# Two RWKV head pairs in one block of the mixer stage, with HGRN on single buffers

## Chip, core and metric

The kernel runs on one core of a Trainium2 chip. The metric is the device time of one execution in microseconds (us); three executions of the kernel before took 3644.89, 3647.28 and 3647.89 us. TensorE (PE) multiplies, VectorE (DVE), ScalarE (ACT) and GpSimd (POOL) work on elements, SyncE (SP) and ScalarE issue most of the transfers. Each engine takes its instructions in program order and waits on semaphores for the others.

## What is computed

One layer of a streaming encoder over 2048 prompt tokens and, with the same weights, 32 sample tokens: a normalised input times one wide weight matrix, whose columns feed three groups of heads side by side (RWKV-7, forgetting attention, HGRN2), then an output projection and a feed-forward network. The change concerns the RWKV group: four heads of 64 channels, whose state is carried from token to token.

```python
xs = p + mu * (p_prev - p)
r, k, v, wl, al, gl = jnp.split(xs, RW_SPLITS, axis=-1)
w = jnp.exp(-jnp.exp(-softplus(-(w0 + tanh(wl) @ w2)) - 0.5))
a = sigmoid(a0 + al @ a2)
g = sigmoid(gl) @ g2
kk = k * k_k, normalised per head
k = k * (1.0 + (a - 1.0) * k_a)
# for each token:
S = S * w_t - (S @ kk_t) (kk_t * a_t) + v_t k_t
y_t = S @ r_t
# then: normalise y per head, add the bonus (r . k . r_k) v, multiply by g
```

(The lines above are shortened from the reference; the transposes and casts are left out.) HGRN2, with four heads too, carries a state in the same way, with a decay per channel and without the correction by `kk`.

## The kernel before

**Stages.** `project_and_recur` runs first, up to about 1300 us: the input projection, the two recurrences, and small work that is strewn in. Behind it stand the attention, the output projection and the feed-forward network, which the change doesn't touch.

**Projection.** Each f32 factor is split into two parts, so a product is three matmuls (L360, L361, L362, tile `ip_p`), 128x128 weights against 256 tokens. The weights arrive as `w_st` (L314, queue of SyncE, two buffers), and are split into `w_hi` (L316, ScalarE) and `w_lo` (L318, GpSimd or VectorE). Results go to the scratch `cm` in HBM, row per channel, column per token. The recurrences read them from there.

**RWKV in half blocks.** `rwkv_block` handles 128 tokens (two chunks of 64) of one pair of heads: 128 partitions are two heads of 64 channels. It is a generator of 34 steps, so that other work can stand between the steps. It loads r, k, v with one extra column and mixes neighbouring tokens (`shifted`, tiles `rw_raw`, `rw_t`, three buffers for `rw_raw`); makes decay and gates from the low-rank tile `rl_e`, which the first pair makes for both (`rwkv_lora`, L1088); takes a running sum (L1111) and exponentials; builds the scaled tiles `rw_G` and `rw_kb`; multiplies them into `rw_gm` (L1151); and inverts a triangular 64x64 matrix per head and chunk, in five levels. At each level a burst of small matmuls (L1201) goes to PSUM, ScalarE copies it to `rw_x` (L1205), a second burst (L1210) uses it, VectorE writes the halves into `rw_tt` under a mask (L993) and transposes to `rw_tn` (L1214), which the next level reads. Then come `rw_wu` (L1221, L1224), `rw_rp` (L1229, L1231), `rw_q` (L1238), the state step per chunk (L1245, L1247), and the output with three sums over heads by the matrix `bones` (L1266, L1272, L1280). All RWKV matmuls write `rw_ps`, three PSUM banks in turn. Nearly all bursts use a part of the array of 64 rows and 64 columns, one part for each head.

**HGRN.** `hgrn_block` handles 256 tokens of one pair in 13 steps. Its tiles `hg_q`, `hg_k`, `hg_b`, `hg_w`, `hg_att`, `hg_vt` have two buffers each, the temporary `hg_t` five.

**Order.** `interleave` takes, again and again, the job with the smallest due time, runs it to its next `yield` and adds the job's step to its due time. A block starts at its number `n`, and takes `RW_LEN / RW_STEPS` units per step; so about three half blocks are under way at a time, each at another step. The projection of the next rounds is a job too and stands between them. The tile framework then sets each engine's order by its own estimate, and puts a semaphore wherever a buffer must come free or a value must be there.

Of the kernel before, what the change touches and what calls it, by code (L numbers as in the profile page):

```python
# [10 lines left out]
F32 = mybir.dt.float32  # L11
# [7 lines left out]
SEQ = 2048  # L19
NS = 32  # L20
# [994 lines left out]
def shifted(K, rp, row, t0, T, n, mu, first, name, bufs=3):  # L1015

    nc = K.nc
    raw = rp.tile([128, T + 1], F32, name="rw_raw", bufs=3)
    if first is None:
        nc.sync.dma_start(out=raw[:, 0:n + 1], in_=K.cm[row:row + 128, t0 - 1:t0 + n])  # L1020
    else:
        if first == 0:
            nc.gpsimd.memset(raw[:, 0:1], 0.0)
        else:
            nc.sync.dma_start(out=raw[:, 0:1], in_=K.a["state_rwkv_shift"][0, 0, 0, row:row + 128].rearrange(
                "(p o) -> p o", o=1))
        nc.sync.dma_start(out=raw[:, 1:n + 1], in_=K.cm[row:row + 128, t0:t0 + n])
    if t0 + n in (SEQ, TOK):
        j = (row - RW0) // 128 + (7 if t0 + n == TOK else 0)
        nc.gpsimd.tensor_copy(K.last[:, j:j + 1], raw[:, n:n + 1])  # L1030
    d = rp.tile([128, T], F32, name="rw_t", bufs=6)
    nc.gpsimd.tensor_tensor(d[:, :n], raw[:, 0:n], raw[:, 1:n + 1], ALU.subtract)
    x = rp.tile([128, T], F32, name=name, bufs=bufs)
# [32 lines left out]
def rwkv_block(K, rp, pp, p, t0, T, n, first, loras, st, yrow):  # L1066
# [10 lines left out]
    if p == 0:  # L1077
        loras[t0] = rwkv_lora(K, rp, t0, T, n, first)
        yield
    lora = loras[t0]  # L1080
    xr = shifted(K, rp, RW0 + 128 * p, t0, T, n, vec(K, "rw_mu", p), first, "rw_r")
    xk = shifted(K, rp, RW0 + 256 + 128 * p, t0, T, n, vec(K, "rw_mu", 2 + p), first, "rw_k")
    xv = shifted(K, rp, RW0 + 512 + 128 * p, t0, T, n, vec(K, "rw_mu", 4 + p), first, "rw_v")
    cs = slice(128 * p, 128 * p + 128)

    def gate(i, bias, name):
        ps = pt()
        nc.tensor.matmul(ps[:, :T], lhsT=K.lw[:, i, cs], rhs=lora, start=True, stop=True)  # L1088
        g = sb(name)
        if bias is None:  # L1090
            nc.scalar.activation(g, ps[:, :T], AF.Copy)
            return g
        nc.vector.tensor_scalar(g, ps[:, :T], bias, -40.0, ALU.add, ALU.max)
        nc.scalar.activation(g, g, AF.Exp, scale=-1.0)
        nc.scalar.activation(g, g, AF.Ln, bias=c1)
        return g

    yield
    nl = gate(0, vec(K, "rw_w0", p), "rw_nl")
    nc.scalar.activation(nl, nl, AF.Exp, scale=-1.0, bias=K.eps_c[:, 2:3])  # L1100
    if n < T:
        nc.gpsimd.memset(nl[:, n:], 0.0)
    yield
    av = gate(1, vec(K, "rw_a0", p), "rw_a")
    nc.scalar.activation(av, av, AF.Exp, scale=-1.0)
    gv = gate(2, None, "rw_g")
# [15 lines left out]
    kk = sb("rw_kk")  # L1122
    nc.scalar.activation(kk, xk, AF.Square, scale=vec(K, "rw_k_k", p))
    ps = pt()
    nc.tensor.matmul(ps[:, :T], lhsT=K.bones, rhs=kk, start=True, stop=True)
    rn = sb("rw_t", bufs=6)
    nc.vector.tensor_scalar(rn, ps[:, :T], 1.0e-24, None, ALU.max)
    nc.scalar.activation(rn, rn, AF.Ln, scale=float(2.0 ** 20))
    nc.scalar.activation(rn, rn, AF.Exp, scale=-0.5, bias=K.rwc[:, 0:1])
    nc.vector.scalar_tensor_tensor(kk, xk, vec(K, "rw_k_k", p), rn, ALU.mult, ALU.mult)  # L1130
    yield

    G = rp.tile([128, 3, NCH, 64], F32, name="rw_G", bufs=3)
# [8 lines left out]
    nc.vector.tensor_scalar(kp, av, vec(K, "rw_k_a", p), K.ka1[:, p:p + 1], ALU.mult, ALU.add)  # L1142
# [6 lines left out]
    for c in range(NCH):  # L1149
        for ps, h in zip(gps, hs):  # L1150
            nc.tensor.matmul(ps[:, 128 * c:128 * c + 128], lhsT=kb[h, c, :, :], rhs=G[h, 0:2, c, :], start=True, stop=True)  # L1151
    for ps in gps:
        v = ps[:, :128 * NCH].rearrange("p (c x) -> p c x", x=128)
        g = rp.tile([128, NCH, 192], F32, name=f"rw_gm{len(gm)}", bufs=2)
        mask = K.m_up.rearrange("p a b -> p (a b)")[:, None, :].broadcast_to([128, NCH, 128])
        nc.vector.tensor_tensor(g[:, :, 0:128], v, mask, ALU.mult)
        gm.append(g)
        if len(gm) == 1:
            m0 = rp.tile([64, NCH, 64], F32, name="rw_m0", bufs=2)
            nc.scalar.activation(m0, g[64:, :, 0:64], AF.Copy)  # L1160
        yield

    kf = kb.rearrange("p c a t -> p c (a t)")
    nc.gpsimd.tensor_tensor(kf, kf, ch(w)[:, :, 63:64].broadcast_to([128, NCH, 128]), ALU.mult)
    ps = pt()
    for c in range(NCH):
        nc.tensor.transpose(ps[:, 128 * c:128 * c + 128], kf[:, c, :], K.ident)
    for i in range(2):
        nc.scalar.activation(gm[i][:, :, 128:192], ps[:, :128 * NCH].rearrange("p (c h x) -> p c h x", h=2, x=64)[:, :, i],
                             AF.Copy)  # L1170
    mt = [m0, gm[1][64:, :, 0:64]]
    kn = rp.tile([128, NCH, 2, 64], F32, name="rw_kn", bufs=2)
    tt = rp.tile([128, NCH, 64], F32, name="rw_tt", bufs=3)
    tn = rp.tile([128, NCH, 64], F32, name="rw_tn", bufs=2)
    flat = lambda t: t.rearrange("p c t -> p (c t)")
    to_tokens(K, pt(), G[:, 0], [kn[h, c, 0, :] for c in range(NCH) for h in hs])
    nc.gpsimd.tensor_copy(tt, K.i2[:, None, :].broadcast_to([128, NCH, 64]))
    for h, m in zip(hs, mt):
        for c in range(NCH):
            by_level(K, tt[h, c, :], 1, halves(m[:, c, :], 1, 1)[:, None], h)  # L1180
    nc.vector.transpose(tn, tt)
    yield

    wu = rp.tile([128, 2, NCH, 2, 64], F32, name="rw_wu", bufs=2)
    to_tokens(K, pt(), ch(xv), [wu[:64, :, c, 1, :] for c in range(NCH)])
    yield

    ps = pt()
    for c in range(NCH):
        for i, h in enumerate(hs):  # L1190
# [962 lines left out]
```

## Time and profile before

| | |
|---|---|
| median of three executions | 3647.28 us |
| profiled execution, whole | 3650.61 us |
| its span, first to last instruction | 3648.6 us |
| instructions | 62814 |
| TensorE busy | 3454.1 us (95%) |
| VectorE busy | 1917.3 us (53%) |
| ScalarE busy | 1486.8 us (41%) |
| GpSimd busy | 1376.2 us (38%) |
| mean granted clock of TensorE | 0.978 |

A row of a group names line, engine, operation, written and read tiles, shape and count; behind the first bar stand the busy time in us and the mean in ns of one, behind the second the idle time of the engine before them and what ended it. A row of waits has the waiting line, what ended the wait, the total in us, how often, and the longest. A row of the timeline has start and duration in us. Matmuls overlap, so the durations of neighbours add up to more than the time that passes.

### The profile page before, as it was taken

The numbers are of one execution on the slowest core, as the hardware profiler recorded it, in microseconds if no ns is written. First come the engines' busy times: TensorE is split into PE (matmuls) and PEld (weight loads), VectorE is DVE, ScalarE is ACT, GpSimd is POOL, SyncE is SP. The second block draws the span as 40 slices with busy tenths as digits, with TensorE's granted clock in tenths as the row PEclk, the third lists the DMA queues.
The fourth block names the chain that finished last, engine by engine and source line by source line (L and its number), as shares of the span: only waits on it lengthen the run. The fifth ranks groups of instructions, "written<-read, shape, count | busy, mean of one in ns | idle before, by whom it ended". The sixth has DMA issues, their size and how long they took to land.

```text
span 3648.6 us, 62814 instructions
## 1 busy us (share of the span) xinstructions
PE 3454.1 (95%) x24242; PEld 2893.4 (79%) x24242; DVE 1917.3 (53%) x4445; ACT 1486.8 (41%) x3492; POOL 1376.2 (38%) x1608
## 2 busy tenths in 40 slices
PE   7999999999999998999999999899999999999999
PEld 5988888888778865666666666688999998998998
DVE  3456667566676555666666655532333345233336
ACT  4356556556566554444444433322122213211212
POOL 5434444344344323544443443333223333322223
PEclk9999999999999999999999999999999999999999
DMA  6433334324533344422222214533222232211212
GB/s 206 144 116 103 96 107 132 119 80 136 185 117 90 103 131 139 124 73 60 75 67 63 75 44 112 176 129 96 63 64 76 71 95 96 70 58 47 70 58 95
DMA packets 363647, 361.37 MB, mean 99 GB/s; under 512 B 36511, under 2 KB 305396, under 8 KB 362292
## 3 DMA queue, kind: packets, MB, share of 16 engines
q1 hardware_dynamic: 325216, 320.02, 29.1%
q10 hardware_dynamic: 37748, 37.29, 3.3%
q8 instruction: 191, 3.13, 0.4%
q14 instruction: 108, 0.88, 0.1%
q0 software_dynamic: 384, 0.05, 0.0%
HBM read 291.14 MB, written 66.14 MB: 98 GB/s over the span
## 4 chain that ended last, share of the span: by engine, by line
PE 72%; DVE 7%; POOL 6%; ACT 6%; DMA 5%; issue 4%; ACTq 0%; SPq 0%; POOLq 0%; DVEq 0%
PE ff_p L1814 8%; PE ff_p L1813 8%; PE ff_p L1812 8%; PE ff_o L1764 4%; PE ff_o L1763 4%; PE ff_o L1762 4%; PE pb_pv L690 4%; PE ip_p L360 3%; PE ip_p L361 3%; PE ip_p L362 3%; PE pb_sc L643 2%; PE pb_ps L706 2%; PE op_p L1672 1%; PE op_p L1671 1%; PE op_p L1670 1%
## 5 line engine op out<-in xcount | busy, mean ns | idle before, releaser
L1813 PE MATMUL ff_p<-h_lo,wih 128*128 128x384 f32 (+2 forms) x1760 | 623.5, 354 | 0.1
L1812 PE MATMUL ff_p<-h_hi,wih 128*128 128x384 f32 (+2 forms) x1760 | 621.6, 353 | 1.9 <-ACT wih L1698 0.8
L1814 PE MATMUL ff_p<-h_hi,wil 128*128 128x384 f32 (+2 forms) x1760 | 622.0, 353 | 1.1 <-POOL wil L1699 1.1
L1699 POOL TENSOR_TENSOR wil<-ff_st,wih 128x1024 fp32r<-128x1024 f32 x134 | 322.3, 2405 | 582.1 <-ACT wih L1698 563.5
L360 PE MATMUL ip_p<-h_hi,w_hi 128*128 128x256 f32 (+1 forms) x1472 | 442.2, 301 | 14.2 <-ACT h_hi L296 5.4
L361 PE MATMUL ip_p<-h_lo,w_hi 128*128 128x256 f32 (+1 forms) x1472 | 429.6, 292 | 4.1 <-POOL h_lo L297 1.9
L362 PE MATMUL ip_p<-h_hi,w_lo 128*128 128x256 f32 (+1 forms) x1472 | 428.3, 291 | 0.3 <-DVE w_lo L318 0.3
L1812 PEld LDWEIGHTS ff_p<-h_hi,wih 128*128 128x128 f32 x1760 | 331.8, 189 | 17.9 <-ACT wih L1698 1.0
L1814 PEld LDWEIGHTS ff_p<-h_hi,wil 128*128 128x128 f32 x1760 | 333.3, 189 | 14.8 <-POOL wil L1699 1.4
L1813 PEld LDWEIGHTS ff_p<-h_lo,wih 128*128 128x128 f32 x1760 | 332.1, 189 | 14.4 <-POOL h_lo L1887 0.6
L1699 POOL TENSOR_TENSOR wol<-ff_st,woh 128x1024 fp32r<-128x1024 f32 x66 | 162.0, 2459 | 406.0 <-ACT woh L1698 405.7
L700 POOL TENSOR_TENSOR fx_acc<-fx_acc,fx_pt 128x512 f32<-128x512 f32 (+3 forms) x176 | 206.5, 1188 | 268.6 <-PE pb_pv L690 152.1
L360 PEld LDWEIGHTS ip_p<-h_hi,w_hi 128*128 128x128 f32 x1472 | 283.6, 193 | 27.5 <-ACT h_hi L296 6.0
L1821 DVE TENSOR_TENSOR ff_sg<-ff_sg,ff_p 128x384 f32<-128x384 f32 (+2 forms) x110 | 64.5, 586 | 458.2 <-PE ff_p L1814 458.0
L1768 DVE TENSOR_TENSOR acc<-acc,ff_o 128x512 f32<-128x512 f32 (+1 forms) x306 | 208.7, 684 | 173.1 <-PE ff_o L1764 172.6
L1762 PE MATMUL ff_o<-woh,act_h 128*128 128x512 f32 (+1 forms) x724 | 286.7, 396 | 10.1 <-ACT act_h L1822 7.2
L361 PEld LDWEIGHTS ip_p<-h_lo,w_hi 128*128 128x128 f32 x1472 | 283.5, 193 | 10.8 <-issue 2.7
L1698 ACT ACTIVATE wih<-ff_st 128x1024 fp32r<-128x1024 f32 x134 | 142.0, 1060 | 366.8 <-PE ff_p L1813 308.8
L362 PEld LDWEIGHTS ip_p<-h_hi,w_lo 128*128 128x128 f32 x1472 | 283.3, 193 | 7.6 <-issue 5.4
L1764 PE MATMUL ff_o<-woh,act_l 128*128 128x512 f32 (+1 forms) x724 | 287.3, 397 | 0.0
L1763 PE MATMUL ff_o<-wol,act_h 128*128 128x512 f32 (+1 forms) x724 | 286.8, 396 | 0.0
L318 POOL TENSOR_TENSOR w_lo<-w_st,w_hi 128x256 fp32r<-128x256 f32 (+2 forms) x220 | 160.7, 760 | 153.1 <-ACT w_hi L316 125.3
(457 smaller groups left out, 7453.0 us busy)
## 6 DMA issues: line engine op xcount, KB each, us to landing
ff_st<-w_ffn_in SPq DMA_DIRECT2D x132, 512.0 KB
w_st<-w_in SPq DMA_DIRECT2D x88, 512.0 KB
ff_st<-w_ffn_out SPq DMA_DIRECT2D x68, 512.0 KB
cm<-ip_e SPq DMA_DIRECT2D x92, 256.0 KB
x_t<-w_ada SPq DMA_DIRECT2D x32, 512.0 KB
fx_kr<-cm SPq DMA_DIRECT2D x80, 128.0 KB
w_st<-w_in SPq DMA_DIRECT2D x16, 520.0 KB
w_a<-w_ada SPq DMA_DIRECT2D x8, 1024.0 KB
```

The lines of the kernel that those rows point to most:

```text
L360: nc.tensor.matmul(ps[:, :T], lhsT=whi[:, d, us], rhs=S.hi[:, d, :T], start=(d == 0), stop=False)
L361: nc.tensor.matmul(ps[:, :T], lhsT=whi[:, d, us], rhs=S.lo[:, d, :T], start=False, stop=False)
L362: nc.tensor.matmul(ps[:, :T], lhsT=wlo[:, d, us], rhs=S.hi[:, d, :T], start=False, stop=(d == ND - 1))
L700: eng.tensor_tensor(acc[i % 2][:m, c0:nq], acc[i % 2][:m, c0:nq], pt[:m, c0:nq], ALU.add)
L1699: nc.gpsimd.tensor_tensor(lo, st, f32(hi), ALU.subtract)
L1762: nc.tensor.matmul(ps[:m], lhsT=ah[:, js], rhs=wh[:, cs], start=(n == 0), stop=False)
L1763: nc.tensor.matmul(ps[:m], lhsT=ah[:, js], rhs=wl[:, cs], start=False, stop=False)
L1764: nc.tensor.matmul(ps[:m], lhsT=al[:, js], rhs=wh[:, cs], start=False, stop=(n == 1))
L1768: nc.vector.tensor_tensor(acc[j][:m, cs], acc[j][:m, cs], ps[:m], ALU.add)
L1812: nc.tensor.matmul(ps[:, :S], lhsT=w[0][:, ds], rhs=hh[:, d, :S], start=(d == 0), stop=False)
L1813: nc.tensor.matmul(ps[:, :S], lhsT=w[0][:, ds], rhs=hl[:, d, :S], start=False, stop=False)
L1814: nc.tensor.matmul(ps[:, :S], lhsT=w[1][:, ds], rhs=hh[:, d, :S], start=False, stop=(d == ND - 1))
```

## The change

A block now holds both pairs: tiles are twice as wide, [pair, chunk, token], so an operation on elements that ran once per pair runs once on twice the columns, and bursts of matmuls go to one PSUM bank for both pairs. Matmuls of 64 columns keep their number and shape. The low-rank tile is made inside the block, the gates of decay and `a` come as one tile of four parts (`rw_ga`), the key's norm is squared from a product that GpSimd makes, token-major copies of `rw_G` and `rw_kb` move in among the levels (`by_tokens`), and the state is one tile for four heads. `rw_rp` is written over `rw_G`. Most tiles have one buffer instead of two or three. The HGRN tiles named above have one instead of two. Due times are given in units of a merged block.

```diff
-def shifted(K, rp, row, t0, T, n, mu, first, name, bufs=3):
+def shifted(K, rp, row, J, t0, T, n, mu, first, name, bufs):
-    raw = rp.tile([128, T + 1], F32, name="rw_raw", bufs=3)
+    raw = rp.tile([128, J, T + 1], F32, name=f"rw_raw{J}", bufs=RAW[J - 1])
+    cols = lambda c0, c1: K.cm[rows, c0:c1].rearrange("(j p) t -> p j t", p=128)
-        nc.sync.dma_start(out=raw[:, 0:n + 1], in_=K.cm[row:row + 128, t0 - 1:t0 + n])
+        nc.sync.dma_start(out=raw[:, :, 0:n + 1], in_=cols(t0 - 1, t0 + n))
...
+RAW, RW_TMP = (1, 2), 4
...
-def rwkv_block(K, rp, pp, p, t0, T, n, first, loras, st, yrow):
+def rwkv_block(K, rp, pp, t0, T, n, first, st):
+    C = T // 64
+    NK, W = 2 * C, 2 * T
...
+    lora = rwkv_lora(K, rp, t0, T, n, first)
+    xk = shifted(K, rp, RW0 + 256, 2, t0, T, n, 2, first, "rw_k", 1)
     yield
+    xr = shifted(K, rp, RW0, 2, t0, T, n, 0, first, "rw_r", 2)
+    xv = shifted(K, rp, RW0 + 512, 2, t0, T, n, 4, first, "rw_v", 2)
+    yield
+    ps = pt()
+    for i in range(2):
+        for j in range(2):
+            nc.tensor.matmul(ps[:, W * i + T * j:W * i + T * j + T], lhsT=K.lw[:, i, 128 * j:128 * j + 128], rhs=lora,
+                             start=True, stop=True)
+    ga = sb("rw_ga", 2, 2 * W)
+    nc.vector.tensor_tensor(pairs(ga, 4), pairs(ps[:, :2 * W], 4), by_pair("rw_w0", 4), ALU.add)
+    nc.vector.tensor_scalar(ga, ga, -40.0, None, ALU.max)
+    nc.scalar.activation(ga, ga, AF.Exp, scale=-1.0)
+    nc.scalar.activation(ga, ga, AF.Ln, bias=c1)
...
+    kk = sb("rw_kk")
+    nc.gpsimd.tensor_tensor(pairs(kk), pairs(xk), by_pair("rw_k_k"), ALU.mult)
+    sq = tmp()
+    nc.scalar.activation(sq, kk, AF.Square)
...
     for h_ in (2, 4, 8, 16, 32):
         ps = pt()
-        for c in range(NCH):
+        for k in range(NK):
             for h, m in zip(hs, mt):
-                nc.tensor.matmul(ps[h, 32 * c:32 * c + 32], lhsT=m[:, c, :], rhs=halves(tn[h, c, :], h_, 0), start=True,
+                nc.tensor.matmul(ps[h, 32 * k:32 * k + 32], lhsT=m[:, k, :], rhs=halves(tn[h, k, :], h_, 0), start=True,
                                  stop=True)
...
+        next(rest, None)
         yield
...
-    for c in range(NCH):
+    for c in range(C):
         ps = pt()
-        for h in hs:
-            nc.tensor.matmul(ps[h, :64], lhsT=rp_[h, c, 1, :], rhs=states[c][h, :], start=True, stop=True)
-        s = rp.tile([128, 64], F32, name=f"rw_s{p}", bufs=5)
+        for j in range(2):
+            for h in hs:
+                nc.tensor.matmul(ps[h, 64 * j:64 * j + 64], lhsT=rp_[h, 1, C * j + c, :], rhs=states[c][h, j, :], start=True,
+                                 stop=True)
+        s = rp.tile([128, 2, 64], F32, name="rw_s", bufs=5)
...
+KB, GM, TT, WU = 1, 2, 1, 1
...
-    sb = lambda name="hg_t", bufs=2: rp.tile([128, T], F32, name=name, bufs=HG_T if name == "hg_t" else bufs)
+    sb = lambda name="hg_t", bufs=1: rp.tile([128, T], F32, name=name, bufs=HG_T if name == "hg_t" else bufs)
-    def load(row, name="hg_t", bufs=2):
+    def load(row, name="hg_t", bufs=1):
...
-                for p in range(2):
-                    jobs.append((n - p * STAG, RW_LEN / RW_STEPS, rw.block(t0, p)))
-                    if t0 % hg.T == 0:
-                        jobs.append((n + p * (hg.T // rw.T - 1) - p * HSTAG + HOFF, HG_LEN / HG_STEPS, hg.block(t0, p)))
-                    n += 1
+                jobs.append((n, RW_LEN / RW_STEPS, rw.block(t0)))
+                if t0 % hg.T == 0:
+                    for p in range(2):
+                        jobs.append((n + p, HG_LEN / HG_STEPS, hg.block(t0, p)))
+                n += 1
...
-RW_LEN, RW_STEPS, HG_LEN, HG_STEPS, IP_LEAD = 3.0, 34, 1.73, 13, 1.0
+RW_LEN, RW_STEPS, HG_LEN, HG_STEPS, IP_LEAD = 1.5, 31, 0.87, 13, 0.5
```

How this moves instructions is seen in the order of TensorE in the second half of the stage. Before, at a place where the second burst of a level (L1210, `rw_tt` and `rw_x` into `rw_ps`) stands beside other half blocks' work (L1088 makes gates, L1245 is a state step, L1058 transposes for HGRN):

```order
L1201 MATMUL rw_ps<-rw_tn,rw_gm_15805 64x32
L1088 MATMUL rw_ps<-rl_e,lw 128x128
L1245 MATMUL rw_ps<-rw_s_15073,rw_rp 64x64 x2
L360 MATMUL ip_p<-h_hi,w_hi 128x256
L1210 MATMUL rw_ps<-rw_tt,rw_x_1455 64x32 x3
L1058 MATMUL hg_ps<-ident,hg_t 128x128
L1210 MATMUL rw_ps<-rw_tt,rw_x_1455 64x32
```

Behind the change, the same burst (now L1239) and the product behind the last level (L1251, `rw_kn` and `rw_tt`), with rows of the modulation (L124) and of the projection between:

```order
L360 MATMUL ip_p<-h_hi,w_hi 128x256
L1239 MATMUL rw_ps<-rw_tt,rw_x_1455 64x32 x3
L124 MATMUL nt_ps<-x_t,sc 32x256 x4
L1239 MATMUL rw_ps<-rw_tt,rw_x_1455 64x32 x5
L361 MATMUL ip_p<-h_lo,w_hi 128x256
L362 MATMUL ip_p<-h_hi,w_lo 128x256
L1251 MATMUL rw_ps<-rw_kn,rw_tt 64x128 x7
```

The burst of four matmuls has become one of eight, and stands half as often.

The transfers that SyncE issues in the middle of the stage. Before, three loads of an RWKV half block stand together, a fourth a little later; `hg_q` and `hg_t` are loads of HGRN, `w_st` weights, `cm` and `tm` results of the projection:

```order
L1361 DMA hg_t<-cm 128x256
L372 DMA cm<-ip_e 128x512
L314 DMA w_st<-w_in 128x4x256
L1361 DMA hg_q<-cm 128x256
L314 DMA w_st<-w_in 128x4x256
L1361 DMA hg_t<-cm 128x256
L1020 DMA rw_raw<-cm 128x129 x3
L397 DMA tm<-ip_e 128x520
L1020 DMA rw_raw<-cm 128x129
```

Behind it, loads of both pairs are one (2x129 columns), the low-rank rows a load of their own (129 columns):

```order
L1022 DMA rw_raw_8378<-cm 128x129
L372 DMA cm<-ip_e 128x512
L314 DMA w_st<-w_in 128x4x260
L1022 DMA rw_raw_7353<-cm 128x2x129
L910 DMA x_t<-cm 128x512
L314 DMA w_st<-w_in 128x4x260
L1022 DMA rw_raw_8391<-cm 128x2x129
L1022 DMA rw_raw_8449<-cm 128x2x129
```

The program has four loads per block of tokens here instead of seven, and the last of a block's four (`rw_raw_7353`, values) stands directly ahead of the next block's keys and receptances.

More of the change, by code (lines that the diff above doesn't have):

```diff
@@ L1028, in shifted @@
+        nc.sync.dma_start(out=raw[:, :, 1:n + 1], in_=cols(t0, t0 + n))
     if t0 + n in (SEQ, TOK):
         j = (row - RW0) // 128 + (7 if t0 + n == TOK else 0)
[L1030 to L1033, printed above, removed]
+        nc.gpsimd.tensor_copy(K.last[:, j:j + J], raw[:, :, n])
+    x = rp.tile([128, J * T], F32, name=name, bufs=bufs)
@@ L1074, in rwkv_block @@
     c1 = K.eps_c[:, 3:4]
     hs = [slice(0, 64), slice(64, 128)]
[L1077 to L1096, printed above, removed]
@@ L1168, in rwkv_block @@
[L1168 to L1176, printed above, removed]
@@ L1177, in rwkv_block @@
[L1177 to L1190, printed above, removed]
-            nc.tensor.matmul(ps[h, 64 * c:64 * c + 64], lhsT=gm[i][:64, c, 0:64], rhs=wu[:64, i, c, 1, :], start=True, stop=True)
@@ L1192, in rwkv_block @@
-    nc.scalar.activation(kn[:, :, 1, :], ch(ps[:, :T]), AF.Copy)
-    yield
+    yield
+    kf = kb.rearrange("p k a t -> p k (a t)")
+    nc.gpsimd.tensor_tensor(kf, kf, ends.broadcast_to([128, NK, 128]), ALU.mult)
+    mt = [m0, gm[1][64:, :, 0:64]]
+    kn = rp.tile([128, NK, 2, 64], F32, name="rw_kn", bufs=1)
+    tt = rp.tile([128, NK, 64], F32, name="rw_tt", bufs=TT)
+    tn = rp.tile([128, NK, 64], F32, name="rw_tn", bufs=1)
+    wu = rp.tile([128, 2, NK, 2, 64], F32, name="rw_wu", bufs=WU)
@@ new lines, in rwkv_block, with tokens @@
+    flat = lambda t: t.rearrange("p k t -> p (k t)")
+    def tokens(src):
+        ps = pt()
+        for j in range(2):
+            nc.tensor.transpose(ps[:T, 128 * j:128 * j + 128], src[:, C * j:C * j + C, :], K.ident)
+        return [ps[64 * c:64 * c + 64, :256].rearrange("p (j h x) -> p j h x", j=2, h=2) for c in range(C)]
+    nc.gpsimd.tensor_copy(tt, K.i2[:, None, :].broadcast_to([128, NK, 64]))
+    for h, m in zip(hs, mt):
+        for k in range(NK):
+            by_level(K, tt[h, k, :], 1, halves(m[:, k, :], 1, 1)[:, None], h)
@@ new lines, in rwkv_block, with by_tokens @@
+    nc.vector.transpose(tn, tt)
+    for c, v in enumerate(tokens(ch(xv))):
+        nc.scalar.activation(wu[:64].rearrange("p h (j c) a x -> p c a j h x", j=2)[:, c, 1], v, AF.Copy)
+    yield
+    nv = pt()
+    for k in range(NK):
+        for i, h in enumerate(hs):
+            nc.tensor.matmul(nv[h, 64 * k:64 * k + 64], lhsT=gm[i][:64, k, 0:64], rhs=wu[:64, i, k, 1, :], start=True, stop=True)
+    nc.scalar.activation(kn[:, :, 1, :], ch(nv[:, :W]), AF.Copy)
+    yield
+    def by_tokens():
+        for c, v in enumerate(tokens(G[:, 0])):
+            for i, h in enumerate(hs):
+                nc.scalar.activation(kn[h].rearrange("p (j c) a x -> p c a j x", j=2)[:, c, 0], v[:, :, i], AF.Copy)
+        yield
+        ps = pt()
+        for k in range(NK):
+            nc.tensor.transpose(ps[:, 128 * k:128 * k + 128], kf[:, k, :], K.ident)
+        for i in range(2):
+            nc.scalar.activation(gm[i][:, :, 128:192], ps[:, :128 * NK].rearrange("p (k h x) -> p k h x", h=2, x=64)[:, :, i],
+                                 AF.Copy)
+        yield
@@ L1264, in rwkv_block @@
     yield
     ps = pt()
-    nc.tensor.matmul(ps[:, :T], lhsT=K.bones, rhs=y, start=True, stop=True)
-    nc.vector.scalar_tensor_tensor(y, ps[:, :T], -1.0 / 64, y, ALU.mult, ALU.add)
-    t1 = sb("rw_t", bufs=6)
+    nc.tensor.matmul(ps[:, :W], lhsT=K.bones, rhs=y, start=True, stop=True)
+    nc.vector.scalar_tensor_tensor(y, ps[:, :W], -1.0 / 64, y, ALU.mult, ALU.add)
+    t1 = tmp()
     nc.scalar.activation(t1, y, AF.Square)
+    for j in range(2):
+        nc.vector.scalar_tensor_tensor(kp[:, js[j]], kp[:, js[j]], vec(K, "rw_r_k", j), xr[:, js[j]], ALU.mult, ALU.mult)
```

212 lines of the change are left out of this document (108 added, 104 removed).

## Prediction

> **What bounds the kernel now.** I read the windows first, to find the stage that the change touches, then the waits of TensorE in it, then the timeline of TensorE at one place, and last the groups by shape for what wider tiles cost. The RWKV tiles are written and read from about 190 to 1270 us. The windows give each engine's busy time and number of instructions for that stretch and the two behind it:
>
> ```profile
> core 0: us, PE busy (x) PEld busy (x) DVE busy (x) ACT busy (x) POOL busy (x), PEclk, DMA share, GB/s
> 190.00:1270.00 1080.00, 1025.46 (x11479) 888.38 (x11477) 698.10 (x2364) 655.93 (x2091) 447.01 (x877) 0.98 0.39 115
> 1270.00:1400.00 130.00, 110.82 (x664) 82.74 (x664) 72.87 (x210) 68.22 (x136) 30.87 (x52) 0.88 0.54 154
> ```
>
> TensorE (PE) is idle for 54.5 us of 1080. VectorE (DVE) is busy 65%, ScalarE (ACT) 61%, GpSimd (POOL) 41%, and the DMA engines 39%. So TensorE sets the pace here. A faster VectorE or ScalarE is worth only what TensorE waits for them. The waits of TensorE between 190 and 1310 us, longest first:
>
> ```profile
> PE rw_ps L1210 <- ACT rw_x L1205: 9.6, 16, 1.5
> PE rw_ps L1201 <- DVE rw_tn L1214: 8.9, 13, 1.1
> PE rw_ps L1151 <- DVE rw_kb L1144: 4.9, 5, 2.0
> PE rw_ps L1221 <- DVE rw_tt L993: 4.4, 4, 2.4
> PE rw_ps L1229 <- ACT rw_wu L1224: 4.3, 4, 3.2
> ```
>
> The five longest are all hand-offs inside an RWKV block, 32.1 us together. They are few: 16 of the 160 full hand-offs at L1210 (the x160 of L1205 below) wait visibly. But a busy TensorE is not one at its peak, since the listed ends overlap. What a matmul really takes is the distance between starts. The timeline of TensorE alone, at a place where a burst of RWKV matmuls cuts into the projection (L360 to L362):
>
> ```profile
> 609.98 0.28 PE L360 MATMUL ip_p<-h_hi,w_hi 128*128 128x256 f32 x1
> 610.10 0.28 PE L361 MATMUL ip_p<-h_lo,w_hi 128*128 128x256 f32 x1
> 610.22 0.28 PE L362 MATMUL ip_p<-h_hi,w_lo 128*128 128x256 f32 x1
> 610.42 0.42 PE L1210 MATMUL rw_ps<-rw_tt,rw_x 64*64 64x32 f32 x8
> 610.78 0.38 PE L360 MATMUL ip_p<-h_hi,w_hi 128*128 128x256 f32 x1
> 611.00 0.28 PE L361 MATMUL ip_p<-h_lo,w_hi 128*128 128x256 f32 x1
> 611.12 0.28 PE L362 MATMUL ip_p<-h_hi,w_lo 128*128 128x256 f32 x1
> ```
>
> The column behind the operands is the part of the array that is used. Projection matmuls follow each other at 0.12 us (609.98, 610.10, 610.22). The one before the burst holds the engine 0.20 us (610.22 to 610.42), the first one behind it 0.22 us (610.78 to 611.00). Inside such a burst the pairs for the two heads follow at 0.06 us:
>
> ```profile
> 608.39 0.22 PE L1201 MATMUL rw_ps<-rw_tn,rw_m 64*64 64x32 f32 x1
> 608.40 0.22 PE L1201 MATMUL rw_ps<-rw_tn,rw_gm 64*64 64x32 f32 x1
> 608.45 0.22 PE L1201 MATMUL rw_ps<-rw_tn,rw_m 64*64 64x32 f32 x1
> ```
>
> The eight matmuls of L1210 are four pairs, 0.24 us, yet 0.36 us pass between 610.42 and 610.78. **An excursion into a burst so costs 0.08 + 0.12 + 0.10 = 0.30 us beside its work:** about 0.10 us for each change of array shape, of which it has two, and 0.10 us for the first projection matmul behind it. This cost, counted as busy, is what the change can take away.
>
> **The change part by part.** *Bursts.* A half block now opens 29 PSUM tiles; the merged block opens 28, each with twice the matmuls of 64 columns. Over the program that is 991 RWKV bursts before and 481 behind. They were often neighbours, so I count in the order of the two programs, from the first to the last RWKV matmul, what costs time: changes of array shape fall from 1053 to 764, runs of projection matmuls from 427 to 358. 289 x 0.10 + 69 x 0.10 = 36 us less. The ends: nothing, if each gap only exposes a wait that lay beneath it; 510 x 0.30 = 153 us, if every burst that goes had been an excursion of its own, which 427 runs exclude. I take the count, 36.
>
> The Trainium skill, TensorEngine Tiling (Array Packing), Key Properties under Tiling Modes, says that changing the tiling mode, not just the tile, drains TensorE. It gives no price. By that rule only the 289 changes of shape would count and the sum would gain 29 us in place of 36; the 0.22 us of the first projection matmul, a full-array one behind a full-array one, speaks for the larger term.
>
> *Matmul work.* The sums over heads by `bones` (L1125, L1266, L1272, L1280) become one matmul of 256 columns in place of two of 128, so 68 fewer instructions with the same columns streamed: 0. The products of 64 columns keep their number.
>
> *Hand-offs.* There are half as many, and each is wider. The groups by shape in this stretch (busy us, mean ns behind the bar) show what width costs:
>
> ```profile
> L1205 ACT ACTIVATE rw_x<-rw_ps 128x64 f32<-128x64 f32 x160 | 35.3, 220 | 44.3 <-PE rw_ps L1201 37.1 <-POOL rw_y L1284 4.8 <-PE rw_ps L1058 0.8
> L1192 ACT ACTIVATE rw_kn<-rw_ps 128x128 f32<-128x128 f32 x32 | 8.9, 277 | 7.1 <-PE rw_ps L1229 4.0 <-PE rw_ps L1191 1.4 <-POOL rw_t L1032 1.0
> L993 DVE COPY_PREDICATED rw_tt<-lev_up,rw_ps 128x64 f32<-128x64 uint32 x160 | 37.8, 236 | 38.4 <-PE rw_ps L1210 37.6 <-PE hg_ps L1058 0.2
> L1214 DVE STREAM_TRANSPOSE rw_tn<-rw_tt 128x128 f32<-128x128 f32 x128 | 38.9, 304 | 1.4 <-DVE ip_e L325 0.2
> L1214 DVE STREAM_TRANSPOSE rw_tn<-rw_tt 128x64 f32<-128x64 f32 x8 | 1.9, 236 | 0.1
> L1231 DVE TENSOR_TENSOR rw_rp<-rw_ps,rw_G 128x256 f32<-128x256 f32 x32 | 13.4, 419 | 20.0 <-PE rw_ps L1229 19.7
> ```
>
> A copy of a level grows from 220 to about 277 ns. The predicated copy and the transpose grow by an estimated 0.06 and 0.14 us (the transpose gained 68 ns from 64 to 128 columns, so twice that for 128 more). That is 0.26 us per level beside TensorE's own bursts. Against it stands the pace: the stretch holds 34 half blocks (16 blocks of tokens and the sample, two pairs each), so a unit of the job list is 1080 / 34 = 31.8 us; a half block has 34 steps in 3.0 units, 2.8 us a step, a merged one 31 steps in 1.5 units of 63.5 us, 3.1 us. The slack grows about as much as the work. I put a wait at one and a half times its old length and half as many of them: 32.1 x 0.75 = 24, so 8 us less. Ends: all 32 gone; or four times the wait, 32 us more. The gates' chain is longest: an addition and a maximum on VectorE and two ScalarE passes on 128x512, not shown before. Four 128x256 passes at about 0.42 are its floor, twice that its ceiling, 1.7 to 3.4 us. Its reader stands two steps on, 6 us. Cost nothing; without that cover at most 17 x 1.7 = 29 us, within the upper end.
>
> *Other engines.* Counted in the two programs, VectorE loses 492 of 4445 instructions, ScalarE 589 rows of its order, GpSimd 150 of 1608 instructions; their time was covered by TensorE and stays so. GpSimd gains one product of 128x256 per block for the key norm; by its row of that width it is 17 x 0.69 = 12 us of an engine idle for 633:
>
> ```profile
> L1405 POOL TENSOR_TENSOR hg_x<-hg_b 128x256 f32<-128x256 f32 x30 | 20.6, 686 | 0.0
> ```
>
> *Single buffers.* HGRN's six named tiles and most RWKV tiles go from two or three buffers to one. An HGRN block lasts 0.87 units of 63.5 us in 13 steps of 4.2 us, and the next begins at 1.0. `hg_q` is last read two steps before the end, so its reload may be issued 0.13 x 63.5 + 2 x 4.2 = 17 us before it is due. A load that was waited for on the chain took this long:
>
> ```profile
> 550.62 3.84 DMA rw_raw<-cm
> ```
>
> 17 us covers 3.84, cost nothing. The third RWKV load of a block (values) must wait until the first (keys) has been consumed; SyncE (SP) waits there with weight loads behind it, as it does already:
>
> ```profile
> SPq L314 <- POOL w_lo L318: 95.5, 33, 5.3
> SPq L1020 <- DVE rw_tn L1181: 62.2, 11, 11.9
> ```
>
> The weight loads at L314 themselves come 95.5 / 33 = 2.9 us early, and TensorE shows no wait for a weight among the long ones. If that cover went, see the last rival.
>
> *Tail.* 58 projection matmuls now stand behind the last RWKV one, 58 x 0.12 = 7 us that move from one full stretch into the next, where TensorE is idle 19 us of 130. I count 0; between 7 less and 7 more. The order of TensorE over its last 9306 instructions is the same.
>
> **Sum.** The profiled execution took 3650.6 us, 2.0 around its span. 3650.6 - 36 - 8 = 3606.6. It lay 3.3 above the median, so 3603 us on the median's scale. Own range 3585 to 3632.
>
> **Rivals.** *More is gained.* If the shorter queues on VectorE (698 us less a fifth) and ScalarE empty the waits altogether, 36 + 32 + 7 go: 3572. For it: TensorE's waits sit behind exactly those two. Against: 1.5 blocks in flight in place of three leave less other work to fill a gap.
>
> *No change, the width is given back.* With 1.5 blocks, a step that waits has nothing behind it but projection, and TensorE takes its work in order. If the 32.1 us grow to 68, the gain is gone: 3647. That needs more than four times the old wait per hand-off, (68 - 16) / 481 = 0.11 us more at each burst. That the merge fails to thin out the bursts can be excluded from the order.
>
> *Slower: HGRN without second buffers.* If the reader of `hg_q` comes within 3.84 us of the last reader of the block before, VectorE, in order, stands for that landing once per block, and the matmuls behind it too: 18 blocks x 3.84 = 69 us against 44 gained: 3672. It decides once the lead falls from 17 us below 3.8, as when SyncE is held by another load in front of it; the wait of 11.9 above shows that this occurs, and 2.9 us of weight lead do not cover it. The Trainium skill, Trainium Kernel Development and Optimization, Best Practices, speaks for this one: it tells to double-buffer so that DMA and compute overlap. By that rule the sum would be this rival's; among the 115 longest pieces of the chain between 190 and 1400 us the 3.84 us above is the only load of a mixer, so far the trace doesn't bear it out.
>
> **How the numbers follow.** Forecast 0.60, more gained 0.17, given back 0.11, slower 0.12. Single measurements here lie within 0.1% of each other, and 0.2% (7 us) is about what can be told from no change: faster means below 3640. Faster 0.77, same 0.11, slower 0.12. The range 3570 to 3645 leaves out the slower case, and part of the two others, about 0.2.
>
> **What would show it.** The RWKV stretch ends near 1225 us in place of 1270, and the stretches behind it keep their length. About 770 changes of shape, with 0.20 and 0.22 us around a burst as before. Waits of TensorE for RWKV tiles sum to 15 to 35 us. SyncE shows waits at the load of `hg_q`, and VectorE none for it. I am wrong if waits for `rw_tn`, `rw_x` or the gates exceed 60 us, or if TensorE waits for weights, `hg_x` or a load.

## The result, and the profile after

| | median, us | range, us (runs) | ratio to before, 95% interval |
|---|---|---|---|
| before | 3646.92 | 3634.96 to 3657.45 (20) | |
| after | 3658.97 | 3640.48 to 3675.74 (20) | 1.0034 [1.002, 1.0047] |

The change makes the kernel about 12 us slower, 0.34%; the forecast was 3603 us. The profiled execution of after is its fastest run (3640.48 us), so its trace shows the change at its best. Of the cores view, the line of before and then that of after (span and mean granted TensorE clock):

```profile
core 0: 3648.6 us, clock 0.978
```

```profile
core 0: 3638.8 us, clock 0.974
```

The windows of after, for the two stretches shown of before:

```profile
190.00:1270.00 1080.00, 996.44 (x11398) 874.70 (x11397) 662.46 (x1885) 575.21 (x1481) 453.76 (x757) 0.96 0.39 116
1270.00:1400.00 130.00, 110.55 (x637) 80.98 (x636) 76.82 (x215) 64.77 (x129) 25.55 (x31) 0.90 0.50 147
```

VectorE and ScalarE have less to do, as planned, yet TensorE is idle 83.6 us in place of 54.5, at a clock of 0.96 in place of 0.98. A fixed window mixes what the RWKV work costs with where it ends. So here is the same view from the first RWKV matmul of each kernel to its last, before and then after:

```profile
172.10:1273.70 1101.60, 1044.67 (x11634) 905.55 (x11633) 712.67 (x2412) 665.61 (x2118) 455.82 (x893) 0.98 0.39 115
```

```profile
170.30:1248.20 1077.90, 997.60 (x11436) 875.40 (x11435) 668.35 (x1905) 576.58 (x1486) 450.43 (x745) 0.97 0.39 116
```

Busy time fell by 47.1 us, of which 7 are the 58 projection matmuls that now come later. The idle time rose from 56.9 to 80.3 us. The stage ends at 1248 us, not near 1225.

Busy time itself depends on the clock, so I split the stretch once more, from the records of TensorE and of its clock: busy time as it would be at full clock, what half clock adds (half of the busy time inside the stretches at half clock), and idle time. Before it is 1023.1 + 21.5 + 56.9 us, after 961.5 + 36.0 + 80.3 us. By this estimate the stretch has 62 us less work for TensorE, the 7 that moved among them, and gives back 15 to the clock and 23 to waiting.

From its end to the first matmul of the feed-forward part, before and then after:

```profile
1273.70:1484.00 210.30, 184.38 (x1022) 136.44 (x1020) 122.02 (x310) 103.16 (x191) 69.06 (x83) 0.93 0.46 135
```

```profile
1248.20:1478.50 230.30, 197.40 (x1104) 145.78 (x1103) 128.09 (x321) 107.70 (x201) 75.08 (x87) 0.93 0.43 129
```

20 us of the gain go here, 13 of them busy time and 7 idle time; all that stands behind is 4 us shorter than before. The waits of TensorE between 190 and 1310 us, after:

```profile
PE rw_ps L1205 <- ACT rw_wu L1199: 12.7, 11, 4.2
PE rw_ps L1299 <- ACT rw_y L1296: 9.2, 6, 2.1
PE rw_ps L1205 <- DVE rw_gm L1169: 9.2, 6, 2.9
PE rw_ps L1165 <- DVE rw_kb L1158: 8.0, 7, 3.1
PE rw_ps L1307 <- ACT rw_t L1302: 5.2, 3, 2.4
...
PE rw_ps L1230 <- DVE rw_tn L1243: 3.6, 2, 3.3
...
PE rw_ps L1239 <- ACT rw_x L1234: 1.3, 2, 1.0
```

The levels (L1230, L1239), whose waits led the list of before, are not among the longest now. The long ones stand at the values' copy and the mask (L1205), the output part (L1299, L1307) and the keys (L1165, 8.0 us where before had 4.9). And they are long: counted from TensorE's records, from 190 us to the last RWKV matmul, waits of over 1 us rose from 15 (22.6 us) to 32 (56.8 us).

One of them, on the timeline of after. VectorE alone first:

```profile
916.45 0.41 DVE L1300 SCALAR_TENSOR_TENSOR rw_y<-rw_ps,rw_y 128x256 f32<-128x256 f32 x1
916.78 0.41 DVE L1147 TENSOR_TENSOR rw_G<-rw_kk,rw_ga 128x256 f32<-128x256 f32 x1
...
920.09 0.89 DVE L1316 TENSOR_SCALAR rw_y<-rw_y,vt 128x128 f32<-128x128 f32 x2
...
922.98 1.13 DVE L1040 SCALAR_TENSOR_TENSOR rw_k<-rw_t,vt,rw_raw 128x128 f32<-128x128 f32 x1
924.04 0.27 DVE L1053 TENSOR_SCALAR rl_e<-rl_x,lsc 128x128 f32<-128x128 f32 x1
924.23 1.27 DVE L1169 TENSOR_TENSOR rw_gm<-rw_ps,m_up 128x512 f32<-128x512 f32 x2
```

Then ScalarE and TensorE, with the idle time before an instruction and its releaser in brackets:

```profile
924.35 0.40 ACT L1054 ACTIVATE rl_e<-rl_e,lsc 128x128 f32<-128x128 f32 x1 [5.32 <-DVE rl_e L1053]
...
925.99 0.77 ACT L1199 ACTIVATE rw_wu<-rw_ps 64x256 f32<-64x256 f32 x2
```

```profile
926.40 0.27 PE L1205 MATMUL rw_ps<-rw_wu,rw_gm 64*64 64x64 f32 x2 [2.25 <-ACT rw_wu L1199]
```

VectorE never rests: the output of one block (L1300, L1316) alternates with the gates' products and the keys of the next (from L1147), then come the mixing of a later block's loads (L1040, L1053), which the framework set here, and the mask (L1169). HGRN has its share between them. ScalarE, in order, stands 5.32 us for a product of L1053, and its copy of the values comes 2.25 us late for TensorE. What follows stands in the windows of the stretch before and of the next 6.8 us:

```profile
915.00:924.00 9.00, 9.00 (x96) 7.25 (x94) 9.00 (x26) 2.05 (x5) 4.16 (x5) 1.00 0.25 69
927.10:933.90 6.80, 6.72 (x53) 5.24 (x50) 2.40 (x10) 0.96 (x3) 0.73 (x2) 0.50 0.55 183
```

Behind the wait TensorE runs at half clock: projection matmuls, which follow each other at 0.12 us otherwise, start 0.21 us apart.

```profile
929.43 0.41 PE L362 MATMUL ip_p<-h_hi,w_lo 128*128 128x256 f32 x1
929.64 0.41 PE L360 MATMUL ip_p<-h_hi,w_hi 128*128 128x256 f32 x1
```

Between 190 and 1270 us before has 6 such half-clock stretches, 41 us long together; after has 13, 82 us, and 12 of them begin during a wait of TensorE of 1.1 us or more, or less than 2 us behind its end. Such moments make up 11% of the time. Over the 20 runs of after time and clock go together: 3640.5 us at 0.974, 3675.7 at 0.964, and span x clock is 3539 to 3553 in all. That product, about the time a run would take at full clock if TensorE always sets the pace, is 3565 for before at a clock of 0.978.

### The profile page after: what moved, and what is told of

It reads as the page before. It is cut to its first block, busy times and chain, and to the rows that moved or that the text cites. A ratio compares the mean times of both kernels' runs of the same rounds, so it can differ in the third digit from the quotient of the medians.

```text
span 3638.8 us, 61058 instructions
## 1 busy us (share of the span) xinstructions
PE 3412.3 (94%) x24106; PEld 2868.6 (79%) x24106; DVE 1880.8 (52%) x3953; ACT 1399.3 (38%) x2865; POOL 1381.2 (38%) x1458
## 4 chain that ended last, share of the span: by engine, by line
PE 61%; DVE 7%; POOL 4%; DMA 3%; ACT 3%; issue 3%; ACTq 0%; POOLq 0%; SPq 0%; DVEq 0%
PE ff_p L1853 8%; PE ff_p L1854 8%; PE ff_p L1852 8%; PE ff_o L1803 4%; PE ff_o L1804 4%; PE ff_o L1802 4%; PE pb_pv L690 3%; PE pb_sc L643 2%; PE pb_ps L706 2%; POOL fx_acc L700 2%; PE op_p L1712 1%; PE ip_p L360 1%; PE pb_ps L707 1%; PE op_p L1711 1%; PE op_p L1710 1%
## 5 line engine op out<-in xcount | busy, mean ns | idle before, releaser
L360 PEld LDWEIGHTS ip_p<-h_hi,w_hi 128*128 128x128 f32 x1472 | 287.6, 195 | 31.2 <-DVE ip_e L325 7.7
```

The costliest lines, as they stand in the source:

```text
L360: nc.tensor.matmul(ps[:, :T], lhsT=whi[:, d, us], rhs=S.hi[:, d, :T], start=(d == 0), stop=False)
```

## The experiments

In the tables, the product is the median over runs of span x clock, and "over 1 us" sums, in us, TensorE's waits longer than that from 190 us to the last RWKV matmul of the profiled run (before: 22.6). `b_` kernels start from before, `a_` kernels from after.

**Repeats, and the single buffers alone.**

```diff
-    sb = lambda name="hg_t", bufs=2: ...
+    sb = lambda name="hg_t", bufs=1: ...
-    def load(row, name="hg_t", bufs=2):
+    def load(row, name="hg_t", bufs=1):
```

> The kernel before, unchanged, to see the granted clock of many of its executions beside the changed kernel's. If the changed kernel's loss is one of clock: span times clock of each kernel is about constant, before near 3648.6 x 0.978 = 3568 us and changed near 3545, and the mean clock of before lies 0.005 or more above the changed kernel's 0.964 to 0.974. If the clock has nothing to do with it: both have the same mean clock, about 0.97, and the ratio to before is 1.000 in any case.

> The changed kernel, unchanged, for a second profile (the first came from its fastest execution) and its clocks on the same chip as the others. Loss by clock: median clock about 0.969, span times clock about 3545, ratio 1.002 to 1.005, and stretches of half clock in the RWKV stage that each follow a wait of TensorE of about 1 us or more. Otherwise: the waits of TensorE alone, some 84 us in the stage, tell the slower executions from the faster ones, and half-clock stretches lie anywhere.

> The kernel before with the HGRN tiles on one buffer, nothing else. Single buffers are the cause: slower by 0.3% or more (3658 us and up), with VectorE or TensorE waiting for hg_q, hg_att or hg_vt. Lead of 17 us covers it: within 0.1% of before, SyncE alone waits for hg_w.

| kernel | median us (runs) | ratio, 95% interval | clock | product | over 1 us |
|---|---|---|---|---|---|
| b_again | 3646.0 (12) | 1.0005 [0.9992, 1.0017] | 0.978 | 3566 | 27.1 |
| a_again | 3653.1 (12) | 1.0026 [1.0009, 1.0043] | 0.971 | 3546 | 56.7 |
| b_hg1 | 3649.2 (12) | 1.0014 [0.9999, 1.0029] | 0.9775 | 3566 | 26.1 |

The loss repeats, and so does its clock, as the forecast for a loss by clock had it: 0.971, product 3546, and 14 of 16 half-clock stretches begin in or right behind a wait. HGRN's single buffers in the kernel before cost at most 0.3% by the interval, by the medians 3 us against b_again and 4 against before, between what was put for the two cases; the product does not move. SyncE's longest waits at the loads of HGRN in after:

```profile
SPq L1401 <- POOL hg_t L1516: 51.2, 10, 9.9
SPq L1401 <- DVE hg_w L1493: 20.7, 10, 3.6
```

The first is at loads into `hg_t`, which has five buffers in both kernels; only the second, at the loads of `hg_q`, can come from the single buffers. VectorE waits for an HGRN load once in the stage, for 0.2 us. So at most a part of the loss is theirs, and a_len17 below gains with them. The RWKV tiles that went to one buffer were not tried by themselves.

**More steps in a block, over a longer time.** The first theory was that steps with too much in them, twice as wide as before, make the waits. This kernel adds four yields (each mask of `rw_gm` its own step; one ahead of the value tokens, one ahead of the keys, one behind the copy of `rw_y`) and spreads 35 steps over 1.7 units:

```diff
-RW_LEN, RW_STEPS, HG_LEN, HG_STEPS, IP_LEAD = 1.5, 31, 0.87, 13, 0.5
+RW_LEN, RW_STEPS, HG_LEN, HG_STEPS, IP_LEAD = 1.7, 35, 0.87, 13, 0.5
```

> The changed kernel with four more yields: one mask of rw_gm per step, the first level apart from the token copies of the values, rw_G apart from rw_kb, and an empty step behind rw_y; 35 steps in 1.7 units, so the same pace per step. Crowded steps are the cause: waits of TensorE in the stage fall from 84 us to 50 or less, fewer half-clock stretches there, mean clock 0.975 or more, 15 to 35 us faster than the changed kernel, so 3625 to 3645. The width of single operations or the small number of blocks under way is the cause: no change, 3650 to 3665.

It took 3603.9 us, 21 us below the range put for this theory. That edit did two things, so the next four take them apart: the length alone; two yields each at 1.6 units; all four at the old 1.5.

> The changed kernel with blocks spread over 1.7 units and no new yield: 31 steps, 3.5 us a step in place of 3.1, and as many blocks under way as with the four yields. If the number of blocks under way (or the longer block) made the gain: about 3604 us as with the yields. If it is what a crowded step holds: the crowded steps keep their work and get 13% more room, waits of 70 to 80 us, 3635 to 3655.

> Two of the four yields alone, those ahead of L1205 (one mask of rw_gm per step; first level apart from the value tokens), 33 steps in 1.6 units. The waits at L1205 were 22 us of 84, the largest; if crowding there is the main cause, they vanish and most of the 49 us comes, 3605 to 3625. If the gain lies in the other two: 3640 or more.

> The other two yields alone (rw_G apart from rw_kb, an empty step behind rw_y), 33 steps in 1.6 units. The waits at L1165 and L1299 were 17 us; with them 10 to 25 us go, 3630 to 3645. If a longer block alone helps: the same as with the first two.

> All four yields, but in 1.5 units: 35 steps of 2.7 us, no more blocks under way than in the changed kernel. If splitting the crowded steps is what counts, most of the gain stays, 3605 to 3630. If room per step or blocks under way counts, it is back at 3640 or above.

| kernel | yields, units | median us (runs) | ratio, 95% interval | clock | product | over 1 us |
|---|---|---|---|---|---|---|
| a_y_len15 | 4, 1.5 | 3658.7 (11) | 1.0029 [1.0018, 1.004] | 0.969 | 3542 | 55.9 |
| a_y12 | 2, 1.6 | 3631.5 (6) | 0.9961 [0.9946, 0.9977] | 0.9745 | 3536 | 49.1 |
| a_y34 | 2, 1.6 | 3620.7 (5) | 0.9923 [0.9911, 0.9935] | 0.976 | 3533 | 38.8 |
| a_len17 | 0, 1.7 | 3611.0 (6) | 0.9901 [0.9884, 0.9918] | 0.9735 | 3513 | 37.9 |
| a_yields | 4, 1.7 | 3603.9 (4) | 0.989 [0.9867, 0.9914] | 0.9755 | 3513 | 27.6 |

The theory of crowded steps fell: the yields alone gain nothing, and one changed number, 1.5 to 1.7, gains 42 us against a_again. The two kernels at 1.6 units lie outside what either theory had for them. The waits of a_len17 in the stage begin

```profile
PE rw_ps L1277 <- DVE rw_s L1280: 7.2, 4, 2.8
PE rw_ps L1239 <- ACT rw_x L1234: 6.9, 10, 2.1
PE rw_ps L1165 <- DVE rw_kb L1158: 6.7, 6, 2.3
```

and those at L1205, L1299 and L1307 are gone from the longest. Its windows from the first to the last RWKV matmul:

```profile
167.90:1222.20 1054.30, 990.92 (x11464) 870.39 (x11463) 674.24 (x1909) 578.46 (x1486) 443.15 (x746) 0.97 0.39 119
```

Idle 63.4 us, and the end at 1222 us, where the forecast had it (1225).

**Which part of a block the time is good for.** The divisor 31 counts a few steps more than a block has, which yields 28 times. So by the due times a block's output part falls 1.26 to 1.36 units behind its start, on the next block's key norm, keys and mask (1.24 to 1.39). At 1.7 units it falls at 1.43 to 1.54, and those at 1.27 to 1.44, so that they barely meet. The timeline above shows them collide at one place. A `yield` with a number lets a step count that often. One kernel pauses four step times ahead of the output part, one pauses as long ahead of the gates, where both parts shift together. A third stretches the blocks of the kernel before, a fourth goes on to 1.8 units with the four yields.

```diff
         states.append(s)
-        yield
+        yield 1 if c < C - 1 else 5
```

```diff
     xv = shifted(K, rp, RW0 + 512, 2, t0, T, n, 4, first, "rw_v", 2)
-    yield
+    yield 5
```

```diff
-RW_LEN, RW_STEPS, HG_LEN, HG_STEPS, IP_LEAD = 3.0, 34, 1.73, 13, 1.0
+RW_LEN, RW_STEPS, HG_LEN, HG_STEPS, IP_LEAD = 3.4, 34, 1.73, 13, 1.0
```

> The changed kernel at its own pace per step (1.5 units for 31 steps), with one pause of four steps' time behind the state loop: the output part of a block comes 0.2 units later, the block takes about 1.7 units. No step has more room than in the changed kernel. Phase theory (what hurts at 1.5 units is that a block's output part falls on the gates, keys and mask of the next): the gain of 1.7 units comes back, 3600 to 3625 us, ratio to before 0.995 or less, TensorE idle in the stretch 190 to 1270 us below 65 us. Room theory (what helps at 1.7 units is 0.055 units a step in place of 0.048): 3643 to 3665 us, as the changed kernel. Length theory (only how long a block lasts counts): 3600 to 3625 us here as well.

> The counterpart of the late pause: the same pause of four steps' time, now between a block's loads and its gates. The block again takes about 1.7 units and no step has more room, but its output part lies on the next block's gates, keys and mask as in the changed kernel, since both come 0.2 units later. Phase theory: no gain, 3643 to 3665 us, ratio to before 1.000 to 1.006. Room theory: 3643 to 3665 us too. Length theory: 3600 to 3625 us. So the pair of pauses tells the three apart: late only, neither, or both.

> The kernel before with its blocks over 3.4 units of one pair in place of 3.0 (the 1.7 units of the changed kernel, in its own units). If longer blocks help whatever the tiles, it gains 0.4% or more: below 3632 us. If the collision is one of the merged block at 1.5 units, the kernel before stays within 0.2%: 3639 to 3654 us. Slower than 3654 us would say that 3.0 was its own best.

> The changed kernel with four more yields and blocks over 1.8 units in 35 steps, the next point behind 1.7 (3603.9 us). If the gain is a matter of phase, it is level or turns back between 1.7 and 1.8: 3598 to 3615 us. If more room a step goes on helping at the same rate as from 1.6 to 1.7 (20 to 25 us per 0.1 unit), 3580 to 3590 us.

| kernel | units | median us (runs) | ratio, 95% interval | clock | product | over 1 us |
|---|---|---|---|---|---|---|
| a_late | 1.7 | 3632.0 (6) | 0.9961 [0.9949, 0.9974] | 0.9725 | 3530 | 48.4 |
| a_early | 1.7 | 3649.3 (12) | 1.0009 [0.9996, 1.0022] | 0.9645 | 3519 | 51.5 |
| b_len34 | 3.4 | 3667.5 (5) | 1.0057 [1.0045, 1.007] | 0.974 | 3572 | 33.3 |
| a_y18 | 1.8 | 3627.6 (5) | 0.9952 [0.9939, 0.9964] | 0.973 | 3529 | 42.7 |

Late helps, early does not, as the collision theory has it. But the late pause brings only half of what 1.7 even units bring, outside what I had put for any theory, and TensorE is idle 78 us between 190 and 1270 us where that theory had less than 65. Here is TensorE's time from the first to the last RWKV matmul, split as above, in one profiled run of each (that of a_early is the second slowest of its twelve):

| kernel | stretch, us | busy at full clock | added by half clock | idle |
|---|---|---|---|---|
| before | 1101.5 | 1023.1 | 21.5 | 56.9 |
| after | 1077.8 | 961.5 | 36.0 | 80.3 |
| a_again | 1083.5 | 962.0 | 40.5 | 80.9 |
| a_late | 1065.0 | 964.7 | 24.6 | 75.7 |
| a_early | 1088.8 | 953.5 | 60.6 | 74.7 |
| a_len17 | 1054.3 | 959.7 | 31.2 | 63.4 |
| a_yields | 1045.8 | 965.2 | 21.4 | 59.1 |

The two pauses leave about the same idle time; what parts them is the clock. a_early has the lowest clock of all kernels, with 22 half-clock stretches in the window from 190 to 1270 us, and by its product it saved more than a_late. Why it draws so many is open. So the pair does not show the collision. Its waits speak half for it, half against:

```profile
PE rw_ps L1239 <- ACT rw_x L1234: 13.3, 13, 2.5
PE rw_ps L1205 <- ACT rw_wu L1199: 12.0, 8, 2.9
```

Those at L1205 are still there, as they should be, but those at L1299 and L1307 are gone from the longest here too. Length is no gain of its own: the kernel before loses 21 us by it, and 1.8 units lose 24 against 1.7 with the same yields, outside both ranges put for that kernel; its longest waits, 21.6 us, stand at the second burst of the levels. The waits of a_late begin

```profile
PE rw_ps L1165 <- DVE rw_kb L1158: 21.2, 12, 3.1
PE rw_ps L1239 <- ACT rw_x L1234: 11.4, 10, 2.6
```

Those at L1205, L1299 and L1307 are off the list, as the collision theory wants, and the keys and the levels have taken their place. My reading was that the next block has less work of TensorE beside it while a block pauses. Between a block's key norm and its keys TensorE works 7.7 us on average in a_late and 8.3 us in after; but in a_early it is 7.2 us, with 2.8 us of such waits in all. So that is not the whole of it.

**The keys beside the pause.** a_late_kb is a_late with a yield ahead of the keys; a_len16 is after with its length alone at 1.6.

> The late pause (3632.0 us) with one yield more, between the gates' products and the keys. With the pause, TensorE's waits for the next block's keys rose to 21.2 us in 12 waits, while those for the values' copy and the output part went; the reading is that a pause takes work away from the steps that lie beside it, which then are too short for the seven VectorE operations of that step. If so, a second step for them brings the waits for the keys below 10 us and the time to 3610 to 3625 us. If the rest that the pause does not gain has nothing to do with that step, it stays at 3626 to 3640 us, and the wait turns up in the levels (now 11.4 us).

> The changed kernel with its length alone at 1.6 units (31 steps, no yields), between 1.5 (3653 to 3659 us) and 1.7 (3611.0 us). If the length alone sets the time and the yields add little, 3622 to 3638 us, about the middle, and at least as slow as the two kernels of 1.6 units with two yields each (3631.5 and 3620.7 us). If it is a threshold between two pieces of work that meet or miss each other, it lies at one of the ends: below 3616 or above 3645 us.

The added yield changed next to nothing in TensorE's own order there (on average 47 projection matmuls in place of 46 between a block's key norm and its keys), so that run said nothing on its question. a_late_kx puts 57 there, by counting the keys' step four times and the pause's four, and TensorE works 10.6 us between the two. a_y34_17 is the pair of yields that did best at 1.6, at 1.7.

```diff
     nc.vector.tensor_tensor(kb[:, :, 0, :], ch(kp), ch(wi), ALU.mult)
 
-    yield
+    yield 4
```

> The late pause with a real increase of the work beside the keys: the added yield of the run before put 47 in place of 46 projection matmuls between a block's key norm and its first use of the keys, that is nothing, so that run said nothing on its question. Here the step behind the keys counts four times (three more step times) and the pause before the output part four (three more), some 1.79 units in all; 57 projection matmuls stand there, 10 x 0.12 = 1.2 us more for each block. If the second half of the gain is the room for the keys: waits for them fall from 21.2 us below 10, and the time from 3632 to 3612 to 3624 us. If the second half lies in the even spread over all steps: the waits for the keys fall but others take their place, 3626 to 3642 us.

> The two yields that did best at 1.6 units (between the gates' products and the keys, and behind the copy of the output), at 1.7 units in 33 steps. Length rules and yields add little: 3598 to 3612 us, level with the kernel of four yields at 1.7 (3603.9 us) and with none (3611.0 us). If these two yields add their 4 to 10 us of 1.6 units again: 3594 to 3602 us. Above 3615 us would say that 1.7 is no plateau.

| kernel | median us (runs) | ratio, 95% interval | clock | product | over 1 us |
|---|---|---|---|---|---|
| a_late_kb | 3631.6 (12) | 0.9973 [0.996, 0.9987] | 0.970 | 3524 | 40.3 |
| a_len16 | 3624.4 (6) | 0.9953 [0.9937, 0.997] | 0.976 | 3535 | 40.0 |
| a_late_kx | 3620.3 (6) | 0.9933 [0.9918, 0.9949] | 0.972 | 3517 | 37.7 |
| a_y34_17 | 3604.8 (5) | 0.9888 [0.9871, 0.9905] | 0.974 | 3513 | 38.8 |

With work beside them, the waits for the keys vanish from the list of a_late_kx, which begins

```profile
PE rw_ps L1239 <- ACT rw_x L1234: 14.1, 12, 3.0
PE hg_ps L1459 <- DVE hg_x L1449: 8.1, 5, 2.6
PE rw_ps L1230 <- DVE rw_tn L1243: 7.2, 10, 2.0
```

and the time falls 12 us. Two places of the block, given time, make 33 of the 42 us, in a block of 1.79 units; the levels still wait. Length alone goes 3653, 3624, 3611 us at 1.5, 1.6 and 1.7: gradual, no threshold, though a_y12 at 1.6 is 7 us slower with its two yields. Three kernels at 1.7 units, with 0, 2 and 4 yields, lie within 7 us, and all beat both kernels; the best, a_yields, by 1.1%.

## Why the prediction was wrong

*What bounds the stage: right on the whole.* From the first to the last RWKV matmul of after TensorE is busy 93% of the time and VectorE 62%. At single places, such as 915 to 924 us, VectorE is busy without a gap, and the wait of TensorE that follows is set there.

*Bursts, 36 us less: right in direction, and too small.* Busy time fell by 47 us less 7 moved, 40, with more of it at half clock. At full clock it would be 62 less 7, some 55 us, by the split above.

*Hand-offs, 8 us less: the step that failed.* It went: "The slack grows about as much as the work. I put a wait at one and a half times its old length and half as many of them". Idle time in the stage grew by 23 us in its place, and the waits over 1 us by 34 us (56.8 against 22.6), 29 us of it back at 1.7 units with four more yields (27.6 left). Two things were wrong in it. It scaled the waits that before had, most of them at the levels, and those did shrink; the long ones stand where before had none or few. And it reckoned slack per step, 3.1 against 2.8 us, as if each step had it to itself. At 1.5 units the output of one block, the keys and mask of the next and the mixing of a later one's loads share VectorE, and TensorE takes its matmuls in order: the timeline shows it at one place. That the pace is at fault is shown by the one number that was changed; that it acts by this collision is argued. The signs of error that the forecast named, waits for `rw_tn` and `rw_x` over 60 us, did not come: they were some 7 us.

*The rivals.* "The width is given back" expected about the time of before, with 0.11, by 0.11 us more at each burst; what came are few and long waits. The slower case, with 0.12, had VectorE stand for the loads of `hg_q`, which it does for 0.2 us.

*The clock: not considered.* The forecast priced a wait at its own length, and took single measurements to lie within 0.1%; the 20 runs of before spread by 0.6%, those of after by 1.0%. The clock at the median of after was 0.969 in place of 0.978. At 0.978 its product of 3545 would be 3625 us; so the clock goes with some 30 us.

*Single buffers, 0: right within the measurement,* 3 to 4 us by b_hg1. SyncE waits at the load of `hg_q`, 20.7 us, and VectorE next to nothing, as the forecast said it would show.

*Tail, 0 with 7 to either side: too small.* In the profiled runs the part behind the last RWKV matmul took 16 us more. The 58 projection matmuls were foreseen at 7 us; the 7 us of idle time and the rest of the busy time were not.

*The sum.* On the profile's scale the forecast was 3606.6 us, and the profiled run of after took 3640.5: 34 us more. Hand-offs missed by 31 us, half clock by 15 and the tail by 9; the bursts gave 19 more than forecast, and the stage begins 2 us earlier. The other 22 of the 56 us come from comparing medians: the profiled run of after is its fastest, at a clock of 0.974, the one of before was 3 us above its median. With blocks over 1.7 units the merge brings 3604 to 3611 us. That this meets the forecast of 3603 is luck: the work saved at the bursts is larger than forecast there too, and the idle time of the stretch is 59 to 63 us, above the 57 of before and not 8 below it.

*What stays open:* how much of the loss at 1.5 units is the collision itself and how much the clock that goes with it; why the late pause and the early one differ so much in clock with about as much waiting; what the single buffers of the RWKV tiles cost by themselves; and whether the place of HGRN's blocks beside those of RWKV matters, since no run moved these alone. Nor was before tried with blocks shorter than 3.0 units.

## What to carry to other kernels

When blocks in flight are merged into fewer, wider ones, the pace has to be set anew: vary the one number that spreads a block, before judging the merge. Beside the slack per step, look at which parts of neighbouring blocks lie beside each other on the second engine, and count TensorE's long waits, and its time at half clock, apart from the rest. And check what work really lies beside a step: a yield that puts no matmul there gives it no time.

## What was not expected of the hardware

Waits of 1 to 3 us seem to cost more than themselves. Between 190 and 1270 us of after, 12 of 13 half-clock stretches of 3.4 to 17.1 us begin in or right behind a wait of 1.1 to 4.2 us, and 14 of 16 in a_again; in before and b_again it is 9 of 16. A stretch of 6.8 us, like the one at 927 us, takes 3.4 us of TensorE's time. Not every such wait draws one: after had 32 over 1 us up to its last RWKV matmul. Nearly the same total of waits over 1 us (48.4 and 51.5 us) went with 27.3 and 63.1 us lost to half clock in the profiled runs of a_late and a_early. The Trainium skill, TensorE: Matmul & The Clock Gate, HAM oscillation, gives as its abstract rule that TensorE should have no idle gaps of over about 3.4 us. All but one of these waits of after, that of 4.2 us, lie below that, and the trace differs. The Trainium skill, TensorE: Matmul & The Clock Gate, What's actually happening, tells of a free-running window of about 3.4 us. The stretches here, of 3.4, 6.8, 10.2 and 17.1 us, agree: they are one, two, three and five times as long.

A kernel's runs then spread with its clock (0.964 to 0.974 over the 20 runs of after, 1% in time), and a single profiled run may show a gain that the median does not have.
